# Releasing half of the first weight quarter behind a small copy, and other spins, in the opening of a decayed cumulative sum of a matmul

## The chip, the cores and the metric

The kernel runs on one core of one Trainium2 chip. The metric is the device time of one execution in microseconds, as the median of several runs. TensorE is called PE here, VectorE DVE, ScalarE ACT, GpSimd POOL and SyncE SP. A DMA transfer is issued by SP, ACT or POOL and is carried out by the core's 16 DMA engines; in the profile the queue of POOL is q0, those of SP and ACT are q1 and q10.

## The reference

```python
B, S, D = (16, 2048, 1024)
x = randn(B, S, D)          # float32
w = randn(D, D)             # float32
decay = 0.9 * rand(D) + 0.05

xw = x @ w
out[:, 0, :] = xw[:, 0, :]
for t in range(1, S):
    out[:, t, :] = decay[None, :] * out[:, t - 1, :] + xw[:, t, :]
```

A matrix product with a 1024 x 1024 weight, and then along the time axis a first-order recurrence with one decay for each output channel.

## The kernel before

**Tiling.** The 1024 channels that are summed over are cut into K = 8 blocks of 128, called k. The time axis of each of the 16 batches is cut into 4 chunks of 512 steps, so there are 64 chunks, two to a group. The 1024 output channels are cut into 8 tiles, called n. For each n and chunk the PE sums 8 matmuls of 128x128 weights and 512 columns into PSUM; ACT, DVE and POOL then work out the recurrence with scans, DVE turns the result round by 32x32 transposes, and SP stores it. These steps form one long list that is written out by hand, the agenda; letters stand for deeds, and every instruction is kept in program order on its engine.

**x.** A chunk of x is loaded from POOL with a conversion from float32 to bf16 (L105): four transfers for each piece, one for every quarter q of the channels, each into 32 partitions. Four transposes on DVE (L115, letter E in the opening), one for each m = 0 to 3, bring the channels to the partitions. A transpose delivers a pair of blocks, k = 2m and k = 2m + 1, interleaved. The matmuls of even k read the interleaved tile xw directly at first; those of odd k read a separated copy, xt, made by ACT (G) or DVE (F) at L123.

**w.** The weight is loaded in four quarters (h, e): h is the half of the output channels (0: n = 0 to 3), e the parity of k. A quarter holds the four row sets m = 0 to 3, row set m being block k = 2m + e. The first quarter, (0, 0), is loaded in float32 by two transfers on SP and two on ACT, 256 KB each, one for every channel quarter q, each with all four row sets (`load_w`, L317 to L322). The other three quarters are loaded from POOL with conversion to bf16 (letter U, 128 KB written by each transfer). A row set is then copied, and for the first quarter converted, into its place in wsb by `settle` (L326): letter W on DVE, w on ACT. The numbers 0 to 3 behind these letters are the row sets of (0, 0), 4 to 7 those of (0, 1).

**The opening** (agenda entry -99) runs in this order. POOL issues M0 (x's first chunk, time blocks 0 to 9 of 16), U0 (the second quarter of w), M1 (the rest of x's first chunk), M2 and M3 (the two halves of the second chunk), then U1 and U2 (the third and fourth quarter of w). The order of the other engines' work is that of the agenda's string:

```python
-99: "M0 U0 M1 M2 M3 U1 U2 w0 W1 w2 W3 K3 E0 E1 G0 E2 G1 E3 F2 G3 W4 w5 W6 W7 E4 ...
```

The first real matmuls are those of M0's 320 time steps for n = 0 to 3: sixteen for k = 0, 2, 4, 6, then sixteen for k = 1, 3, 5, 7, and the same for the 192 steps of M1. They need E0 and row set 0 first, then E1 and row set 1, and so on; the odd blocks need U0's row sets (W4, w5, W6, W7) and the copies G and F.

**The spins.** Before any data is there the PE runs matmuls on zeros into a PSUM tile that is overwritten later. `spin(5, seed, wide)` makes five float32 matmuls of 512 columns, each two passes in the profile. Their weights, seed, are zeroed by DVE, and one column of seed is then written by ACT from wide, so the spins start behind that copy. K3 (`spin_on`, L355 to L357) makes one bf16 spin behind the landing of channel quarter 3 of M0: an ACT copy of one column of that quarter into gate, and a matmul with gate as weights.

Of the kernel before, what the change touches and what calls it, by code (L numbers as in the profile page):

```python
# [9 lines left out]
FP32 = mybir.dt.float32  # L10
BF16 = mybir.dt.bfloat16
# [3 lines left out]
def _ap(ap_obj: bass.AP, new_ap, extra_offset=0):  # L15
    return dataclasses.replace(
        ap_obj,
        ap=[list(p) for p in new_ap],
        offset=ap_obj.offset + extra_offset,
    )  # L20
# [5 lines left out]
def kernel(  # L26
# [26 lines left out]
    nc = tc.nc  # L53
    pin = tc.keep_in_program_order
    B, S, D = x.shape
    assert w.shape == (D, D)

    NQ = 4
    P = 32
    CQ = D // NQ  # L60
    K = CQ // P
    M = K // 2
# [3 lines left out]
    R = K // 2  # L66
    CH = D // 2
    CR = CH // NQ

    const = ctx.enter_context(tc.tile_pool(name="const", bufs=1))  # L70
# [9 lines left out]
    def quad(q):  # L80
        return slice(q * P, (q + 1) * P)
# [12 lines left out]
    def ot_tile(nj):  # L94
        return ring(sb, "ot", 4, [128, nj, CR])
# [45 lines left out]
    class Tile:  # L141
# [45 lines left out]
        def copy(self):  # L187
            self.xs = sb.tile([128, 2 * TL], FP32, name=f"xs{self.lot % 3}")[:, 0:self.T]
            size = self.T // len(self.parts())
            for i, ps in enumerate(self.parts()):  # L190
                pin(nc.scalar.copy(out=self.xs[:, i * size:(i + 1) * size], in_=ps))  # L191
# [94 lines left out]
    class Outlet:  # L286
# [8 lines left out]
        def store(self, b, t0):  # L295
# [4 lines left out]
            for j in range(0, self.nj, nj):  # L300
# [8 lines left out]

    room = [ot_tile(2 * NJ).rearrange("p j c -> p (j c)") for _ in range(2)]  # L310
    size = M * CH
    stage = {(0, 0): room[0][:, 0:size],
             (0, 1): room[0][:, size:size * 3 // 2].bitcast(BF16),
             (1, 0): room[1][:, 0:size // 2].bitcast(BF16),
             (1, 1): room[1][:, size // 2:size].bitcast(BF16)}

    def load_w(queues, h, e):  # L317
        for i, q in enumerate((0, 2, 1, 3)):
            pin(queues[i % len(queues)].dma_start(  # L319
                out=stage[h, e][quad(q)].rearrange("p (m d) -> p m d", m=M),  # L320
                in_=_ap(w, [[2 * D, P], [2 * P * D, M], [1, CH]],
                        (q * CQ + e) * D + h * CH)))  # L322

    def settle(h, e, m, copy):
        src = stage[h, e][:, m * CH:(m + 1) * CH]
        pin(copy(out=wcols[:, 2 * m + e, h],  # L326
                 in_=src.rearrange("p (q r i) -> p q r i", q=NQ, r=R)))

    wide = const.tile([128, TL], FP32, name="wide")
    idle = wide[:, 0:TL // 2].bitcast(BF16)  # L330
    spare = ring(psp, "spare", 1, [128, TL])
    rows = const.tile([128, 2, P], FP32, name="rows")
    seed = const.tile([128, 128], FP32, name="seed")
    load_w((nc.sync, nc.scalar), 0, 0)
    pin(nc.vector.memset(wide, 0.0))
    pin(nc.vector.memset(seed, 0.0))
    pin(nc.scalar.copy(out=seed[:, 0:1], in_=wide[:, 0:1]))  # L337

    gate = const.tile([128, 128], BF16, name="gate")
    pin(nc.vector.memset(gate, 0.0))  # L340

    def spin(count, by, on):
        for _ in range(count):
            pin(nc.tensor.matmul(out=spare, lhsT=by, rhs=on, start=True, stop=True))  # L344

    spin(5, seed, wide)
    H = NJ // 2
    cuts = (((0, H + 2), (H + 2, NJ)), ((0, H), (H, NJ)))
    cols = const.tile([128, 2, P], FP32, name="cols")
# [9 lines left out]
    def load_part(i):  # L359
        load_w((nc.gpsimd,), *((0, 1), (1, 0), (1, 1))[i])  # L360
# [4 lines left out]
    def settle_one(i, copy):  # L365
        settle(i // 8, i // 4 % 2, i % 4, copy)
# [119 lines left out]
    def turn_and_load(c):  # L486
# [42 lines left out]
        "L": lambda i: load(*loads.pop(0)) if loads else None,  # L529
    }  # L530
    agenda = {
        -99: "M0 U0 M1 M2 M3 U1 U2 w0 W1 w2 W3 K3 E0 E1 G0 E2 G1 E3 F2 G3 W4 w5 W6 W7 E4 E5 G4 E6 G5 E7 F6 G7 R E8 E9 G8 E10 G9 E11 F10 G11 E12 L E13 G12 L E14 G13 E15 L F14 G15 D",
        0: "",
        1: "",
        2: "",
# [220 lines left out]
```

## Time and profile before

| what | value |
|---|---|
| median of 3 runs | 903.48 us (903.07 to 903.52) |
| the profiled execution | 903.32 us |
| its span, first to last instruction | 901.5 us |
| PE busy | 894.6 us, 4211 matmul records |
| DVE, ACT, POOL busy | 825.8, 685.7, 656.8 us |
| transfers of w's first quarter | 4 x 256 KB, 4.6 us (SP) and 4.9 us (ACT) from issue to landing |
| transfers of M0 | 4 x 160 KB, 6.6 us from issue to landing |
| transfers of w's other quarters | 12 x 128 KB, 5.8 us |

Times are microseconds from the start of the span. A row of the timeline gives the start, the time taken, the engine, the line, the operation, what it writes and reads, how many instructions are merged, and in brackets the idle time ahead of it with what ended it. A row of the windows gives the stretch, its length, the busy time of PE, PE's weight loads, DVE, ACT and POOL with the number of instructions, the granted clock, the share of the DMA engines and their rate in GB/s. A row of a DMA queue gives its packets, the MB written and the time of its packets as a share of the 16 engines' time. x and the later quarters of w are read as float32 and written as bf16, so the bytes read are twice those that the rate shows.

### The profile page before, as it was taken

The page shows a single profiled execution, that of the slowest core. Times are in us where ns is not written, and L with a number is a line of the kernel's source. Part 1 is how long each engine was busy: PE and PEld are TensorE (multiplying, and loading weights), DVE is VectorE, ACT ScalarE, POOL GpSimd, SP SyncE. Part 2 cuts the span into 40 slices and gives each one's busy share as a digit, 9 for nine tenths or more (in the row PEclk, how much of TensorE's full clock was granted, in tenths as well). Part 3 has the DMA queues.
Part 4 walks back from the last instruction along what each step waited for, and adds up shares of the span by engine and source line. Part 5 has one row for each costly group of instructions (what it writes and reads, how often), then busy time and mean ns, then how long its engine had stood idle before and what let it go on. Part 6 is the DMA issues. An engine that isn't in the chain of part 4 may idle for free.

```text
span 901.5 us, 12309 instructions
## 1 busy us (share of the span) xinstructions
PE 894.6 (99%) x4211; PEld 412.8 (46%) x4211; DVE 825.8 (92%) x633; ACT 685.7 (76%) x957; POOL 656.8 (73%) x758
## 2 busy tenths in 40 slices
PE   8999999999999999999999999999999999999998
PEld 5544444444444444444444444444444444444444
DVE  4999989999999999999998999989999999999998
ACT  4888879877877877878778778777787787787743
POOL 7887778877767768677677687777777777776532
PEclk9999999999999999999999999999999999999999
DMA  9999999999999999999999999999999999999658
GB/s 189 192 211 244 244 205 215 215 230 240 248 237 264 242 254 242 256 253 246 220 245 218 228 241 211 239 223 228 236 228 223 229 235 226 230 219 219 187 135 239
DMA packets 403182, 204.77 MB, mean 227 GB/s; under 512 B 9392, under 2 KB 402096, under 8 KB 403120
## 3 DMA queue, kind: packets, MB, share of 16 engines
q0 software_dynamic: 137024, 68.70, 57.5%
q1 hardware_dynamic: 265808, 134.77, 57.1%
q8 instruction: 33, 0.54, 0.2%
q10 hardware_dynamic: 288, 0.52, 0.2%
q14 instruction: 29, 0.24, 0.1%
HBM read 138.42 MB, written 134.22 MB: 302 GB/s over the span
## 4 chain that ended last, share of the span: by engine, by line
PE 99%; ACT 0%; ACTq 0%; DVE 0%; DVEq 0%; issue 0%
PE ps L131 97%; PE spare L131 1%; PE spare L344 1%; ACT L337 0%; PE spare L412 0%; ACTq L319 0%; PE ps L412 0%; DVE h L440 0%; ACT seed L337 0%; DVEq L751 0%
## 5 line engine op out<-in xcount | busy, mean ns | idle before, releaser
L131 PE MATMUL ps<-xt,wsb 128*128 128x512 bf16 (+2 forms) x4040 | 865.9, 377 | 0.0
L131 PEld LDWEIGHTS <-wsb 128*128 128x128 bf16 x4184 | 408.3, 98 | 477.2 <-DVE wsb L326 0.3
L205 POOL TENSOR_TENSOR xs<-h,xs 128x512 f32<-128x512 f32 (+1 forms) x190 | 242.4, 1277 | 185.5 <-ACT h L171 84.4
L191 ACT COPY xs<-ps 128x1024 f32<-128x1024 f32 (+1 forms) x190 | 188.7, 994 | 153.4 <-PE ps L131 147.2
L278 DVE STREAM_TRANSPOSE ot<-so 128x1024 f32<-128x1024 f32 (+2 forms) x264 | 300.6, 1176 | 2.7 <-POOL so L266 2.0
L266 POOL TENSOR_TENSOR so<-h,xs 128x512 f32<-128x512 f32 (+1 forms) x189 | 240.6, 1274 | 38.4 <-ACT h L171 26.2
L123 ACT COPY xt<-xw 128x2048 bf16<-128x2048 bf16 (+3 forms) x136 | 242.4, 1788 | 5.8 <-DVE xw L115 5.8
L105 POOL DMA_DIRECT2D xb<-in_x_dram x264 | 173.8, 659 | 7.6 <-DMA xb<-in_x_dram 2.8
L171 ACT ACTIVATE h<-so,dec 128x512 f32<-128x512 f32 (+1 forms) x189 | 144.7, 766 | 26.6 <-DVE so L210 23.3
L115 DVE STREAM_TRANSPOSE xw<-xb 128x2048 f32<-128x2048 f32 (+3 forms) x78 | 147.2, 1899 | 6.1 <-DMA xb<-in_x_dram 6.1
L210 DVE TENSOR_TENSOR_SCAN so<-spare,keep,xs 128x512 f32<-128x512 f32 (+1 forms) x97 | 120.0, 1240 | 27.5 <-POOL xs L205 26.9
L210 DVE TENSOR_TENSOR_SCAN so<-spare,xs 128x512 f32<-128x512 f32 x93 | 113.3, 1220 | 25.9 <-POOL xs L205 22.6
L171 ACT ACTIVATE h<-ps,dec 128x512 f32<-128x512 f32 (+1 forms) x190 | 129.6, 683 | 0.0
L229 DVE TENSOR_TENSOR_SCAN so<-dec,ps 128x1024 f32<-128x1024 f32 x34 | 76.9, 2261 | 0.8 <-ACT h L171 0.6
L229 DVE TENSOR_TENSOR_SCAN so<-dec,keep,ps 128x1024 f32<-128x1024 f32 (+2 forms) x35 | 75.5, 2156 | 0.8 <-PE ps L131 0.8
L270 ACT COPY keep<-so 128x1 f32<-128x1 f32 x136 | 25.3, 188 | 9.3 <-DVE so L229 8.7
L201 ACT COPY so<-keep 128x1 f32<-128x1 f32 x97 | 18.3, 191 | 3.3 <-DVE ot L278 3.2
L199 POOL MEMSET so<- 128x1 f32 x93 | 10.6, 115 | 3.0 <-DVE ot L278 3.0
L131 PE MATMUL spare<-xt,wsb 128*128 128x512 bf16 (+3 forms) x60 | 12.6, 329 | 0.0
L131 PE MATMUL ps<-xw,wsb 128*128 128x256 bf16 (+3 forms) x72 | 12.2, 306 | 0.0
L344 PE MATMUL spare<-wide,seed 128*128 128x512 f32 x10 | 7.4, 915 | 3.2 <-ACT seed L337 3.2
L319 POOL DMA_DIRECT2D ot<-in_w_dram x12 | 6.5, 548 | 0.7 <-issue 0.3
(43 smaller groups left out, 37.6 us busy)
## 6 DMA issues: line engine op xcount, KB each, us to landing
out_dram<-ot SPq DMA_DIRECT2D x236, 512.0 KB, 8.9
xb<-in_x_dram POOLq DMA_DIRECT2D x248, 256.0 KB, 7.4
out_dram<-ot SPq DMA_DIRECT2D x56, 128.0 KB, 2.2
out_dram<-ot SPq DMA_DIRECT2D x8, 256.0 KB, 4.8
ot<-in_w_dram POOLq DMA_DIRECT2D x12, 128.0 KB, 5.8
xb<-in_x_dram POOLq DMA_DIRECT2D x8, 128.0 KB, 4.5
out_dram<-xb SPq DMA_DIRECT2D x3, 256.0 KB
xb<-in_x_dram POOLq DMA_DIRECT2D x4, 160.0 KB, 6.6
```

What stands on the lines that cost most here:

```text
L105: pin(nc.gpsimd.dma_start(out=xb_of[c][quad(q), j0:j1], in_=_ap(x, [[D, P], [P * D, j1 - j0], [1, CQ]], (b * S + t0 + j0 * P) * D + q * CQ)))
L115: pin(nc.vector.transpose(out=dst.rearrange("p (m j i) -> p j m i", m=M, i=P)[:, j0:j1, m0:m1], in_=src.rearrange("p (j m c) -> p j m c", ...
L123: pin(copy(out=xt_of[c][:, m0:m1, :, j0 * P:j1 * P], in_=src))
L131: return pin(nc.tensor.matmul(out=ps[:, t0 % ps.shape[1]:][:, 0:t1 - t0], lhsT=lhs, rhs=rhs, start=(k == 0 and t0 == start), stop=(k == K ...
L171: pin(nc.scalar.activation(out=h[:, i * size:(i + 1) * size], in_=src, func=mybir.ActivationFunctionType.Copy, scale=dec[:, self.n:self.n ...
L191: pin(nc.scalar.copy(out=self.xs[:, i * size:(i + 1) * size], in_=ps))
L205: pin(nc.gpsimd.tensor_tensor(out=odds, in0=self.g, in1=odds, op=ALU.add))
L210: pin(nc.vector.tensor_tensor_scan(out=so[:, 3:T + 2:2], data0=squares[-1][:, n:n + 1].to_broadcast([128, T // 2]), data1=self.xs[:, 1:T:2 ...
L229: return pin(nc.vector.tensor_tensor_scan(out=so[:, t + 2:t + 2 + size], data0=dec[:, n:n + 1].to_broadcast([128, size]), data1=ps, initia ...
L266: pin(nc.gpsimd.tensor_tensor(out=self.so[:, 2:T + 2:2], in0=self.h, in1=self.xs[:, 0:T:2], op=ALU.add))
L270: pin(nc.scalar.copy(out=self.keep, in_=self.so[:, self.T + 1:self.T + 2]))
L278: pin(nc.vector.transpose(out=outlet.ot[:, :, c0:c0 + P], in_=self.so[:, 2 + t0:2 + t0 + nj * P].rearrange("p (i t) -> p i t", t=P)))
```

## The change

- The loads of the first quarter, (0, 0), are cut in two. Row sets 0 and 1 are issued first, two transfers on SP and two on ACT, of half the size. Row sets 2 and 3 are issued in four more transfers that write the rest of the same tile.
- Between them stands an ACT copy of one zero column from wide into the first column of row set 2's place. The later transfers overwrite that column, so on SP and on ACT they are issued only when the copy is done. The copy takes the place of the one into seed; the tile seed and its memset are gone.
- The spins are four in float32 with `wide[:, 0:128]` as weights, and two in bf16 with gate as weights. They need only DVE's memsets.
- In the agenda K2 is added ahead of K3: one more copy and bf16 spin, behind channel quarter 2 of M0. w2 moves from ahead of K3 to behind K3 on ACT, ahead of G0; W3 moves on DVE from ahead of E0 to behind E3, ahead of F2.

```diff
-    stage = {(0, 0): room[0][:, 0:size],
-             (0, 1): room[0][:, size:size * 3 // 2].bitcast(BF16),
+    early = M // 2
+    rounds = room[0][:, 0:size]
+    stage = {(0, 1): room[0][:, size:size * 3 // 2].bitcast(BF16),
...
-    def load_w(queues, h, e):
+    def staged(h, e, m0, m1):
+        if (h, e) == (0, 0):
+            return rounds[:, m0 * CH:m1 * CH]
+        return stage[h, e][:, m0 * CH:m1 * CH]
+
+    def load_w(queues, h, e, m0=0, m1=M):
         for i, q in enumerate((0, 2, 1, 3)):
             pin(queues[i % len(queues)].dma_start(
-                out=stage[h, e][quad(q)].rearrange("p (m d) -> p m d", m=M),
-                in_=_ap(w, [[2 * D, P], [2 * P * D, M], [1, CH]],
-                        (q * CQ + e) * D + h * CH)))
+                out=staged(h, e, m0, m1)[quad(q)].rearrange("p (m d) -> p m d", m=m1 - m0),
+                in_=_ap(w, [[2 * D, P], [2 * P * D, m1 - m0], [1, CH]],
+                        (q * CQ + e + 2 * P * m0) * D + h * CH)))
 
     def settle(h, e, m, copy):
-        src = stage[h, e][:, m * CH:(m + 1) * CH]
         pin(copy(out=wcols[:, 2 * m + e, h],
-                 in_=src.rearrange("p (q r i) -> p q r i", q=NQ, r=R)))
+                 in_=staged(h, e, m, m + 1).rearrange("p (q r i) -> p q r i", q=NQ, r=R)))
...
-    seed = const.tile([128, 128], FP32, name="seed")
-    load_w((nc.sync, nc.scalar), 0, 0)
+    load_w((nc.sync, nc.scalar), 0, 0, 0, early)
     pin(nc.vector.memset(wide, 0.0))
-    pin(nc.vector.memset(seed, 0.0))
-    pin(nc.scalar.copy(out=seed[:, 0:1], in_=wide[:, 0:1]))
+    pin(nc.scalar.copy(out=rounds[:, early * CH:early * CH + 1], in_=wide[:, 0:1]))
+    load_w((nc.sync, nc.scalar), 0, 0, early, M)
...
-    spin(5, seed, wide)
+    spin(4, wide[:, 0:128], wide)
+    spin(2, gate, idle)
...
-        -99: "M0 U0 M1 M2 M3 U1 U2 w0 W1 w2 W3 K3 E0 E1 G0 E2 G1 E3 F2 G3 W4 w5 W6 W7 E4 ...
+        -99: "M0 U0 M1 M2 M3 U1 U2 w0 W1 K2 K3 E0 E1 w2 E2 E3 W3 G0 G1 F2 G3 W4 w5 W6 W7 E4 ...
```

## The prediction

> **What bounds the kernel now.** I read the shares and the chain first, to see which engine sets the end; then the timeline of the opening; then the half-microsecond windows with the DMA rate, and the queues in single windows.
>
> ```profile
> PE 894.6 (99%) x4211; PEld 412.8 (46%) x4211; DVE 825.8 (92%) x633; ACT 685.7 (76%) x957; POOL 656.8 (73%) x758
> ...
> PE ps L131 97%; PE spare L131 1%; PE spare L344 1%; ACT L337 0%; PE spare L412 0%; ACTq L319 0%; PE ps L412 0%; DVE h L440 0%; ACT seed L337 0%; DVEq L751 0%
> ```
>
> TensorE (PE) is the chain from 3.21 us to the tail. No group of real matmuls has idle time ahead of it that counts, so the end is the start of the first real matmul plus a stream without holes. Only two things can move it: when that stream starts, and holes made in it.
>
> ```profile
> 0.74 0.90 ACTq L319 DMA_DIRECT2D ot<-in_w_dram  x2
> 0.75 0.86 SPq L319 DMA_DIRECT2D ot<-in_w_dram  x2
> ...
> 1.31 2.51 POOL L105 DMA_DIRECT2D xb<-in_x_dram  x4 [0.86 <-POOLq L740]
> ...
> 2.97 0.19 ACT L337 COPY seed<-wide 128x1 f32<-128x1 f32 x1
> ...
> 3.21 7.42 PE L344 MATMUL spare<-wide,seed 128*128 128x512 f32 x10 [3.21 <-ACT seed L337]
> ...
> 7.04 1.14 ACT L326 CAST wsb<-ot 128x512 bf16<-128x512 f32 x2 [3.87 <-DMA ot<-in_w_dram]
> ...
> 10.33 1.69 DVE L115 STREAM_TRANSPOSE xw<-xb 128x320 f32<-128x320 f32 x4 [2.50 <-DMA xb<-in_x_dram]
> ...
> 10.90 0.59 PE L131 MATMUL ps<-xw,wsb 128*128 128x320 bf16 x3
> ...
> 12.94 0.70 DVE L326 COPY wsb<-ot 128x512 bf16<-128x512 bf16 x3 [0.54 <-DMA ot<-in_w_dram]
> ...
> 15.00 1.16 DVE L115 STREAM_TRANSPOSE xw<-xb 128x192 f32<-128x192 f32 x4 [1.36 <-DMA xb<-in_x_dram]
> ```
>
> The reader is to see that the first matmul (10.90) hangs on x's first piece (M0), whose transposes wait for a DMA until 10.33, while w's quarter is there at 7.04, over 3 us before it is needed. Behind it the second quarter of w (12.94) and x's second piece (15.00) also arrive by DMA just when the PE wants them: the hole at 13.29 is 0.15 us, the one at 15.48 nothing. The PE can keep an earlier start only if all these transfers come earlier too.
>
> ```profile
> 3.50:4.00 0.50, 0.50 (x1) 0.21 (x1) 0.00 (x0) 0.00 (x0) 0.50 (x2) 1.00 1.11 377
> 4.00:4.50 0.50, 0.50 (x2) 0.27 (x1) 0.00 (x0) 0.00 (x0) 0.50 (x2) 1.00 0.77 254
> 4.50:5.00 0.50, 0.50 (x1) 0.07 (x1) 0.00 (x0) 0.00 (x0) 0.50 (x2) 1.00 0.83 287
> ...
> 7.00:7.50 0.50, 0.50 (x1) 0.13 (x1) 0.43 (x2) 0.47 (x1) 0.00 (x0) 1.00 1.06 124
> ...
> 8.50:9.00 0.50, 0.50 (x2) 0.33 (x1) 0.00 (x0) 0.00 (x0) 0.20 (x1) 1.00 1.47 196
> ```
>
> The last column is the DMA rate. w runs at 377, dips to 254 and 287 between its two pairs of transfers, and x, alone from 6.5 on, runs at 132, 124, 151 and 160 in four windows before it reaches about 195. By queue, x (q0) moves nothing at all before 5.5, though issued from 1.31 on:
>
> ```profile
> q10 hardware_dynamic: 70, 0.14, 72.6%
> q1 hardware_dynamic: 38, 0.05, 28.6%
> ...
> q0 software_dynamic: 124, 0.06, 92.8%
> ```
>
> (the first two lines are all there is in 5.0 to 5.5, the third is new in 5.5 to 6.0). x starts just as w thins out.
>
> **The change part by part.** *Spins.* They now wait only for the memset of wide (0.92 + 0.48 = 1.40), so they start at about 1.45 instead of 3.21. Before, a pass took 0.85 us until 9.02, some 5.8 us after the first, and 0.43 then. Eight passes with the step 5.8 us after their start: 6.8 x 0.85 + 1.2 x 0.43 = 6.3, so to 7.8; the two bf16 spins at most 0.39 each (the row of the old gate spin), to 8.2 or 8.6. Nothing real waits for them. Their price is nothing as long as the clock stays up until the first real matmul; else see the second rival.
>
> *The copy.* Same instruction, place and 0.19 us, another destination. The removed memset of seed (0.17) had nobody waiting but that copy, which starts behind the table load anyway. Nothing.
>
> *Four more w issues.* Two on ACT behind the copy: 2 x 0.44 from 3.16, to 4.05; ACT then waited until 7.04, so hidden. Two on SP, which waits for the copy: 2 x 0.41; SP's next work is the decay load at 16.5. POOL's queue is not touched. Nothing on either side.
>
> *The moved casts.* On ACT the second cast now stands behind the spin copy at 10.29: 10.5 to 11.1; three copies of 0.66 follow to 13.1 and the next cast (0.62) to 13.7; its matmul ran at 13.85, so 0.13 us to spare. On VectorE (DVE) the fourth cast (0.42) follows the transposes, 12.02 to 12.44, for a matmul at 12.58; the copy behind it ends at 12.89, just ahead of 12.94. Nothing; if these covers were gone, 0.2 us at most (the last ACT cast moves from 12.92 to 13.1). One more spin copy (0.19) and spin (0.39) fall into the wait for x: nothing.
>
> *The transfers* are the one term. The early half of w is 256 packets of 2 KB; summed by quarter microseconds, q1 and q10 had moved 276 packets by 4.0, so it is through at about 3.9. The other half is issued at 3.2; q1's first packet came 1.0 us after its issue and q10's 1.76 us, so it begins at 4.2 and 4.9. That leaves a hole in which x can move, before w's second half joins it. The trace does not show such a hole; its bounds:
> - Gain: what x and w leave unused now. In 4.0 to 5.0, (2 x 375 - 254 - 287) x 0.5 = 104 KB at 375 is 0.28 us. In 6.5 to 8.5, (4 x 195 - 567) x 0.5 = 106 KB at 195 is 0.55 us. Together 0.83. To this the slow first stretch (1.75 to 3.0, 73 packets where the later pace makes 250, some 0.9 us) could add only if restarting cost nothing.
> - Loss: x does not move before 5.5 anyway and w's second half starts as slowly as the first: 73 of its packets by 5.5, 183 left, against about 30 left before. 153 x 2 KB = 0.31 MB, at the 0.39 MB/us that x reads (twice its written 195) 0.8 us if nothing of it fits into the slack of 6.5 to 8.5 (0.55), 0.25 if all does.
>
> I take the gain of 0.83: the nearest row is x's own start, full at once when it comes (18 packets in its first tenth of a microsecond, 40 in its sixth), as of a queue that had been ready and held back. From 8.5 on the same queue carries the second quarter of w and the rest of x at a steady 190 to 207, each transfer let go by the landing of an earlier one, so all arrivals move by the same 0.83 and open no hole.
>
> [...] The trace shows both: 107 packets of q0 beside 105 of q1 in 59.5 to 60.0, and none of q0 beside w before 5.5. This is the third rival's ground.
>
> Sum: the profiled execution took 903.32 (span 901.5 and 1.8 around it); minus 0.83 is 902.49. The median of the runs lies 0.16 above the profiled one: 902.65, called 902.7.
>
> **The rivals.** *1. Restart (the other side).* x starts at 5.5 whatever w does, because it is its own queue that is not ready, and w's second half is then in its way. For it: in 4.0 to 5.0 the engines had room and x took none. Against it: x's full start. Price: the middle of 0.25 and 0.8, +0.5, that is 904.0; it decides from the point where more than 30 w packets are left when x starts.
>
> *2. Clock.* Spins end at about 8.2; x's third landing, which lets the added spin go, came at about 9.2 (issued 2.6, landed 6.6 later), the fourth at 10.1 (3.2 and 6.9); both by 0.8 earlier in the forecast. The PE thus idles in pieces of 0.5 to 1.5 us where before it had one of 0.4. If the clock falls back, the first real matmuls run at half speed until it is up again, 5.8 us by the spins' row: 2.9 lost. On top of the forecast: +2.1, 905.6. Against it: no row here shows a fall. [...]
>
> *3. It changes nothing.* w's second half joins the queue before x gets a turn, or the queues only trade places: +0, 903.5.
>
> *4. Late w.* As x stood behind w, w's second half stands behind x and even behind the next quarter on x's queue. It then lands at about 12.6 with its cast to 13.2, where its matmul ran at 12.02; the matmuls behind come at 14.3 instead of 13.29: +1.0, 904.5. For it: the total hold of one queue over the other before 5.5. Against it: the equal sharing at 59.5.
>
> **How the numbers follow.** Forecast 0.42 (own range 902.0 to 903.3), restart 0.20, clock 0.18, nothing 0.10, late w 0.10. The bar of 0.2% is 1.8 us, about what a measurement of this kernel can tell from no change: 901.67 and 905.29. Faster than that needs 0.83 and all of the slow first stretch: 0.06. Slower: three quarters of the clock (0.14), a third of late w, and a little of restart: 0.19. Within: 0.75. The range runs from 901.9, the forecast with half as much again, to 905.6, the clock's price; beyond it lie half of the clock case and the outer tails.
>
> **What would show it.** Right: q0 packets from about 4.0; the first transposes at about 9.5 and the first real matmul at 10.1 in place of 10.90; second quarter's cast at 12.1, x's second piece at 14.2; no hole in the PE's row. Wrong: q0 still silent to 5.5 (restart, nothing); 320-column matmuls 0.27 us apart instead of 0.14 (clock); a wait of the PE for the moved casts (late w). A start that moves while the arrivals at 12.94 and 15.00 stay would show up as holes and no gain.

## The result and the profile after

The changed kernel took 906.02 us in the median of 12 runs (904.02 to 908.05), the kernel before 903.48 (902.75 to 904.65, 12 runs): a ratio of 1.0028 with a 95% interval of 1.0018 to 1.0038. It is slower by 2.5 us, where 0.8 less was forecast. It also scatters: the three runs with a mean clock of 0.999 or 1.000 took 904.0 to 904.6, the five at 0.997 or 0.998 took 905.4 to 906.3, the four at 0.996 took 907.2 to 908.1. The profiled execution took 905.84 with a span of 904.1, that is 2.6 longer than the span before.

The chain of the changed kernel by engine, on the page:

```profile
PE 98%; DMA 1%; POOL 0%; issue 0%; DVE 0%; ACT 0%; DVEq 0%; ACTq 0%; POOLq 0%
```

and some of its first pieces in order of time (start, time taken, what):

```profile
1.31 1.92 POOL xb L105 x3
3.23 7.79 DMA xb<-in_x_dram
...
11.34 0.39 PE spare L348
11.73 0.91 PE ps L131 x3
```

The fp32 spins are no longer on it; of the spins only the one behind x's last channel quarter (11.34) is. The end now hangs on the last transfer of x's first piece, 7.79 us from issue to landing, and on the PE behind it. The timeline of the opening:

```profile
0.75 3.28 SPq L325 DMA_DIRECT2D ot<-in_w_dram  x4
...
1.46 5.42 PE L348 MATMUL spare<-wide 128*128 128x512 f32 x8 [1.46 <-DVE wide L339]
...
3.19 0.85 ACTq L325 DMA_DIRECT2D ot<-in_w_dram  x2
...
6.71 0.59 PE L348 MATMUL spare<-wide,gate 128*128 128x512 bf16 x2
...
9.80 0.39 PE L348 MATMUL spare<-wide,gate 128*128 128x512 bf16 x1 [2.50 <-ACT gate L361]
...
11.14 1.69 DVE L115 STREAM_TRANSPOSE xw<-xb 128x320 f32<-128x320 f32 x4 [5.90 <-DMA xb<-in_x_dram]
...
11.34 0.39 PE L348 MATMUL spare<-wide,gate 128*128 128x512 bf16 x1 [1.15 <-ACT gate L361]
...
11.71 0.94 PE L131 MATMUL ps<-xw,wsb 128*128 128x320 bf16 x3
...
15.79 1.16 DVE L115 STREAM_TRANSPOSE xw<-xb 128x192 f32<-128x192 f32 x4 [1.35 <-DMA xb<-in_x_dram]
```

Two things to see. The first transposes start at 11.14 instead of 10.33, and the first real matmul at 11.71 instead of 10.90: 0.81 late. And three matmuls of 320 columns take 0.94 where they took 0.59, behind holes of the PE of 2.50 and 1.15 us. The windows show why; the last three columns are the granted clock, the DMA share and GB/s:

```profile
3.50:4.00 0.50, 0.50 (x2) 0.17 (x1) 0.00 (x0) 0.00 (x0) 0.50 (x2) 1.00 0.96 124
...
5.50:6.00 0.50, 0.50 (x3) 0.26 (x2) 0.00 (x0) 0.00 (x0) 0.48 (x1) 1.00 1.07 127
...
7.50:8.00 0.50, 0.00 (x0) 0.00 (x0) 0.00 (x0) 0.00 (x0) 0.37 (x1) 1.00 1.02 241
...
11.50:12.00 0.50, 0.50 (x3) 0.19 (x2) 0.50 (x3) 0.50 (x2) 0.44 (x2) 0.78 1.25 199
12.00:12.50 0.50, 0.50 (x4) 0.26 (x3) 0.50 (x3) 0.50 (x2) 0.50 (x1) 0.50 1.30 193
...
15.00:15.50 0.50, 0.50 (x5) 0.30 (x3) 0.00 (x0) 0.00 (x0) 0.50 (x2) 0.81 1.44 192
```

The clock is at half from about 11.8 to 15.2. The first sixteen real matmuls took 15.57 - 11.71 = 3.86 us to the start of the next block; before, 13.29 - 10.90 = 2.39 with a wait of 0.15 in it, which is gone in the changed kernel. So the profiled execution lost 0.81 by the late start and, with that wait set against it, 1.47 by the clock, 2.28 in all; from 27.7 us to the last DVE work the distance to before stays at 2.23 to 2.24, and 0.36 more lies behind that work, at the very end. Where x moves, by queue (packets, MB, share of the engines), first in 3.25 to 3.50, then in 6.00 to 6.25:

```profile
q0 software_dynamic: 18, 0.01, 26.9%
...
q1 hardware_dynamic: 3, 0.01, 20.4%
```

x does start in the hole, at about 3.3 instead of 5.5. But from 4.0 to 6.0, alone on the engines, it runs at only 126 to 163 GB/s, and w's second half, issued from 3.19 on, brings its first packet only at 6.0, and its last after 10.2.

### The profile page after: what moved, and what is told of

Same layout as the page of the kernel before. It is cut to its first block, busy times and chain, and to the rows that moved or that the text cites. A ratio compares the mean times of both kernels' runs of the same rounds, so it can differ in the third digit from the quotient of the medians.

```text
span 904.1 us, 12321 instructions
## 1 busy us (share of the span) xinstructions
PE 895.0 (99%) x4212; PEld 413.0 (46%) x4212; DVE 825.8 (91%) x632; ACT 685.8 (76%) x958; POOL 657.7 (73%) x758
## 4 chain that ended last, share of the span: by engine, by line
PE 98%; DMA 1%; POOL 0%; issue 0%; DVE 0%; ACT 0%; DVEq 0%; ACTq 0%; POOLq 0%
PE ps L131 97%; PE spare L131 1%; DMA xb<-in_x_dram 1%; POOL xb L105 0%; PE spare L417 0%; PE ps L417 0%; DVE h L445 0%; PE spare L348 0%; ACT gate L361 0%; DVEq L756 0%; ACTq L361 0%; POOLq L745 0%
## 5 line engine op out<-in xcount | busy, mean ns | idle before, releaser
L348 PE MATMUL spare<-wide 128*128 128x512 f32 x8 | 5.4, 836 | 1.5 <-DVE wide L339 1.5
```

## The experiments

Each kernel is the changed one but for the edit shown, unless it says otherwise. "Clock low" counts the executions with a mean clock of 0.998 or less; none of the 86 executions of the kernel before that ran beside these kernels was so low. The last column is that of one execution, the profiled one.

| kernel | median us | range | clock low | first transposes, in its profile |
|---|---|---|---|---|
| before | 903.3 to 903.5 | 902.8 to 904.7 | 0 of 86 | 10.33 |
| changed | 906.02 | 904.0 to 908.1 | 9 of 12 | 11.14 |
| 14 early spins | 904.72 | 904.1 to 905.6 | 0 of 11 | 11.85 |
| whole loads | 903.43 | 903.1 to 904.8 | 3 of 11 | 10.27 |
| old spins | 905.23 | 904.5 to 906.8 | 1 of 11 | 10.63 |
| divided, no wait | 904.92 | 904.3 to 906.6 | 0 of 11 | 12.30 |
| agenda alone | 903.45 | 902.9 to 903.9 | 0 of 11 | 10.14 |
| one spin fewer | 906.12 | 905.7 to 907.7 | 5 of 5 | 10.98 |
| second half behind x | 910.73 | 909.2 to 911.5 | 5 of 5 | 9.23 |
| second half on POOL | 905.97 | 905.5 to 906.8 | 3 of 6 | 9.99 |
| whole loads, 12 spins | 904.05 | 903.3 to 904.3 | 0 of 11 | 10.30 |
| released by DVE | 906.08 | 904.8 to 906.4 | 5 of 6 | 11.37 |
| full-size transfers | 904.82 | 904.1 to 905.8 | 0 of 11 | 11.56 |
| late spins | 905.24 | 904.4 to 907.8 | 3 of 11 | 12.25 |

**14 early spins: the hole filled.**

```diff
-    spin(2, gate, idle)
+    spin(14, gate, idle)
```

> The changed kernel with 14 bf16 spins in place of 2, so that the PE works on until about 9.9 us instead of 7.3. Theory (two costs that add: the clock falls because the PE idles from 7.3 to 9.8 and from 10.2 to 11.3, and x's first piece lands 0.8 us late because w's held-back half comes in beside it): the granted clock stays at 1.00 from the first real matmul on, the first piece still lands late (transposes at about 11.1), so 904.3, and the scatter of 904.0 to 908.1 closes to that of the kernel before. Rival (the clock falls for another reason, the early start of the spins for one): 906.0 and the same scatter.

904.72, a ratio of 1.0013 (1.0004 to 1.0022) to before. The PE's rows:

```profile
6.76 3.19 PE L348 MATMUL spare<-wide,gate 128*128 128x512 bf16 x14
...
10.51 0.39 PE L348 MATMUL spare<-wide,gate 128*128 128x512 bf16 x1 [0.57 <-ACT gate L361]
...
12.41 0.58 PE L131 MATMUL ps<-xw,wsb 128*128 128x320 bf16 x3
```

The work ends at 9.95, the first real matmuls take 0.58 although they begin even later, and no execution has a low clock. So, by the medians, 906.02 - 904.72 = 1.3 of the loss is the clock, and 904.72 - 903.5 = 1.2 is left with the clock up. The three executions of the changed kernel that kept the clock took 904.0 to 904.6; by their middle one, 904.26, it would be 1.8 and 0.8. Which of the two is nearer is not shown: x may have come early in those three, or the added spins may cost something themselves.

**Whole loads: the changed spins without the divided loads.**

```diff
-    load_w((nc.sync, nc.scalar), 0, 0, 0, early)
+    load_w((nc.sync, nc.scalar), 0, 0)
+    seed = const.tile([128, 1], FP32, name="seed")
...
-    pin(nc.scalar.copy(out=rounds[:, early * CH:early * CH + 1], in_=wide[:, 0:1]))
-    load_w((nc.sync, nc.scalar), 0, 0, early, M)
+    pin(nc.scalar.copy(out=seed, in_=wide[:, 0:1]))
```

> The changed kernel's spins and agenda, but w's first quarter is loaded whole and at once as before; the small copy goes to a tile of its own. Theory: x's first piece lands at 10.3 as before, and the PE idles from about 7.3 to 9.4 and 9.8 to 10.5, so the clock falls in many of the executions: 903.5 to 906.9 with a median near 905, scattered. Rival (the held-back half is what costs, through DMA alone): 903.5 and no scatter.

The hole and the first transposes:

```profile
9.66 0.39 PE L348 MATMUL spare<-wide,gate 128*128 128x512 bf16 x1 [2.63 <-ACT gate L361]
...
10.27 1.69 DVE L115 STREAM_TRANSPOSE xw<-xb 128x320 f32<-128x320 f32 x4 [2.73 <-DMA xb<-in_x_dram]
```

903.43, ratio 1.0003 (0.9994 to 1.0011): x is on time, and the whole loss of the median is gone. Three of eleven executions had a clock of 0.998, all at 904.7 to 904.8, the profiled one among them (its windows from 12 to 14 us stand at 0.50). So the spins make the clock fall without the loads too, but less often than expected: the holes are 2.63 and 0.41 us here, and the median stays.

**Old spins: the divided loads with the PE at work.**

```diff
+    seed = const.tile([128, 128], FP32, name="seed")
...
+    pin(nc.vector.memset(seed, 0.0))
...
+    pin(nc.scalar.copy(out=seed[:, 0:1], in_=wide[:, 0:1]))
...
-    spin(4, wide[:, 0:128], wide)
-    spin(2, gate, idle)
+    spin(5, seed, wide)
```

> The changed kernel's loads and agenda, with the five fp32 spins of before behind their own ScalarE copy, from about 3.4 us on. Theory: the PE works until about 10.7, the clock stays at 1.00, and only the late first piece is left: 904.3, no scatter. Rival (everything lies in the clock, and x's lateness was that one execution): 903.5. Rival (smaller transfers or the moved casts cost more than that): 905 or more with the clock at 1.00.

905.23, ratio 1.0020 (1.0011 to 1.0028), nearly a microsecond more than expected with the clock up in ten of eleven. In its profile x was early for a divided load (10.63), but the copy behind the last quarter had to wait for the added spin, which stood behind the fp32 spins until 11.1. That explains a part in that one execution; the rest of the run's scatter was not taken apart.

**Divided, no wait.** Eight transfers at once, the changed agenda, the spins of before.

```diff
+    seed = const.tile([128, 128], FP32, name="seed")
     load_w((nc.sync, nc.scalar), 0, 0, 0, early)
+    load_w((nc.sync, nc.scalar), 0, 0, early, M)
     pin(nc.vector.memset(wide, 0.0))
-    pin(nc.scalar.copy(out=rounds[:, early * CH:early * CH + 1], in_=wide[:, 0:1]))
-    load_w((nc.sync, nc.scalar), 0, 0, early, M)
+    pin(nc.vector.memset(seed, 0.0))
+    pin(nc.scalar.copy(out=seed[:, 0:1], in_=wide[:, 0:1]))
...
-    spin(4, wide[:, 0:128], wide)
-    spin(2, gate, idle)
+    spin(5, seed, wide)
```

> The loads cut in two, but all eight transfers are issued at once with no copy to wait for; the changed kernel's agenda, the spins of before. Theory (it is the wait, not the cut, that delays x): x's first piece lands at 10.3, 903.5. Rival (eight small transfers are slower than four, or the agenda costs): 904.3, as in the run that keeps the wait.

904.92, ratio 1.0017 (1.0009 to 1.0026): the expected 903.5 did not come. The first transposes, and the queues in 4.0 to 4.5:

```profile
12.30 1.69 DVE L115 STREAM_TRANSPOSE xw<-xb 128x320 f32<-128x320 f32 x4 [6.91 <-DMA xb<-in_x_dram]
...
q0 software_dynamic: 37, 0.02, 32.1%
q1 hardware_dynamic: 10, 0.02, 25.8%
q10 hardware_dynamic: 8, 0.01, 6.6%
```

All eight transfers were issued by 2.6, yet by queue only the first two of SP and of ACT ran ahead of x. x moved from 3.5 on, and the other four trickled in beside it: 18 packets in 4.0 to 4.5, 23 in the next half microsecond. The wait is not needed for the harm: here x got in between although all of w's first quarter had been issued, as four smaller transfers on each queue in place of two. The profiled execution (906.17) is one of the slower ones of this kernel.

**Agenda alone**, on the kernel before.

```diff
-        -99: "M0 U0 M1 M2 M3 U1 U2 w0 W1 w2 W3 K3 E0 E1 G0 E2 G1 E3 F2 G3 W4 ...
+        -99: "M0 U0 M1 M2 M3 U1 U2 w0 W1 K2 K3 E0 E1 w2 E2 E3 W3 G0 G1 F2 G3 W4 ...
```

> The kernel before with nothing but the changed agenda: the added copy and spin behind channel quarter 2, and the two moved casts. Theory (the agenda costs nothing by itself): 903.5, x's first piece at 10.3. Rival (the 1.2 to 1.7 us that the runs with divided loads and an unbroken clock lost lie in the moved casts): 904.7 or more.

903.45, ratio 1.0000 (0.9991 to 1.0009). The moved casts, the added copy and spin cost nothing.

**One spin fewer.**

```diff
-        -99: "... w0 W1 K2 K3 E0 E1 ...
+        -99: "... w0 W1 K3 E0 E1 ...
```

> The changed kernel without the added copy and spin behind channel quarter 2, so that the PE idles in one piece from 7.3 to about 11.3. Theory (the length of the idle time decides on the clock): the clock falls in every execution or nearly, and later executions lose up to 3.4 us at half speed: median 906.5 to 907.5, none below 905. Rival (the clock falls whatever the PE does in that time): the same 906.0 and scatter as the changed kernel.

906.12, and every one of five executions at a clock of 0.997 or less, none below 905.66; the hole is 4.21 us. The median is a little under what was expected. In the profiled execution, the fastest of the five, the clock is at half for 3.41 us; the two at 0.996 took 907.5 and 907.7, which fits twice that.

**Second half behind x.** It is released by the landing of x's first piece.

```diff
-    pin(nc.scalar.copy(out=rounds[:, early * CH:early * CH + 1], in_=wide[:, 0:1]))
-    load_w((nc.sync, nc.scalar), 0, 0, early, M)
...
-    spin(2, gate, idle)
+    spin(6, gate, idle)
...
+    def load_late(i):
+        pin(nc.scalar.copy(out=rounds[:, early * CH:early * CH + 1], in_=xb_of[0][:, 0, 0:1]))
+        load_w((nc.sync, nc.scalar), 0, 0, early, M)
...
-        -99: "... W1 K2 K3 E0 ...
+        -99: "... W1 K2 K3 N0 E0 ...
```

> The changed kernel, but w's second half is released only by the landing of all of x's first piece, and there are six bf16 spins. Theory (x is late because w's second half comes in beside it from 6 us on): with x alone on the engines its first piece lands before 10.3, about 9.2, so the first transposes start then; w's second half is then late and the PE waits for its casts, until about 12. Rival (x is late because its own queue starts slowly, whatever comes beside it): transposes at 10.5 or later here too.

Three rows of the timeline and two of the windows:

```profile
9.23 1.69 DVE L115 STREAM_TRANSPOSE xw<-xb 128x320 f32<-128x320 f32 x4 [3.94 <-DMA xb<-in_x_dram]
...
9.62 0.85 ACTq L325 DMA_DIRECT2D ot<-in_w_dram  x2
...
15.83 0.62 ACT L331 CAST wsb<-ot 128x512 bf16<-128x512 f32 x1 [6.24 <-DMA ot<-in_w_dram]
...
4.00:4.50 0.50, 0.50 (x2) 0.32 (x1) 0.00 (x0) 0.00 (x0) 0.50 (x2) 1.00 1.09 137
...
7.50:8.00 0.50, 0.50 (x4) 0.10 (x1) 0.00 (x0) 0.00 (x0) 0.30 (x1) 1.00 1.45 190
```

With x alone its first piece is there at 9.23, 1.1 sooner than before, as expected: it is w's second half beside it that makes x late. But that half, issued at 9.6, was cast at 15.83, not at 12, its first packets coming from about 11.9 on. 910.73: the PE waited 5.4 us, and the clock fell in that wait. SP's first packet of the held half came some 2.3 us after its issue here and ACT's 2.9, against 2.8 and 3.7 in the changed kernel and 1.0 and 1.8 for the first transfers of the kernel before.

**Second half on POOL**, converted on the way, between x's first piece and the second quarter.

```diff
-    pin(nc.scalar.copy(out=rounds[:, early * CH:early * CH + 1], in_=wide[:, 0:1]))
-    load_w((nc.sync, nc.scalar), 0, 0, early, M)
...
-    spin(2, gate, idle)
+    spin(6, gate, idle)
...
+    def load_late(i):
+        load_w((nc.gpsimd,), 0, 0, early, M)
...
-        -99: "M0 U0 M1 ...
+        -99: "M0 N0 U0 M1 ...
```

> The changed kernel with w's second half moved to POOL's queue, behind x's first piece and ahead of the second quarter of w, converted on the way, with six bf16 spins. Theory (one queue in the wanted order does what the change was to do): x's first piece at about 9.2, w's second half by about 10.3, the first real matmul near 9.8; but the second quarter and the rest of x still come through the same engines, so the PE meets holes and the whole gains 0.2 to 0.8: 902.7 to 903.3. Rival (x cannot come earlier): 903.5 or more. Rival (four more transfers on POOL delay the ones behind them, since each waits for an earlier one to land): 904 or more.

905.97. x's first piece came at 9.99, but the last rival held: in the timeline the first eight POOL transfers were issued by 5.9, and each of the four of the second quarter only as one of x's transfers landed (7.59, 8.41, 9.27, 10.15), the DMA rate sank to 116 GB/s in 12 to 13 us, and the PE waited for that quarter:

```profile
10.15 0.54 POOL L327 DMA_DIRECT2D ot<-in_w_dram  x1 [0.33 <-DMA xb<-in_x_dram]
...
15.12 0.62 ACT L333 COPY wsb<-ot 128x512 bf16<-128x512 bf16 x1 [1.32 <-DMA ot<-in_w_dram]
...
15.50 0.58 PE L131 MATMUL ps<-xt,wsb 128*128 128x320 bf16 x3 [1.14 <-DVE wsb L333]
```

No version here beats the kernel before.

**Whole loads, 12 spins.** The run with whole loads, with `spin(12, gate, idle)`.

> Whole loads of w's first quarter at once and the changed agenda, with 12 bf16 spins in place of 2. In the run with two the clock was below 1.00 in some executions and the median was that of the kernel before. Theory (the hole in the PE's work from 7.0 to 9.7 lets the clock fall in some executions): no execution above 904.3 now, median 903.4, clock 1.00 or 0.999 everywhere. Rival (the early start of the spins costs the clock): the same four or so executions of eleven at 904.3 to 904.8.

904.05, ratio 1.0006 (0.9997 to 1.0015). No low clock any more, as expected, so the early start of the spins alone does not make the clock fall. But the spins were too many: in the profile the clock rose late, the fp32 spins took 6.51 us where the changed kernel's took 5.42, the bf16 spins ran to 10.56, and the first real matmul came at 11.74 with x ready at 10.30.

**Released by DVE**, 1.5 us sooner.

```diff
-    pin(nc.scalar.copy(out=rounds[:, early * CH:early * CH + 1], in_=wide[:, 0:1]))
+    pin(nc.vector.tensor_copy(out=rounds[:, early * CH:early * CH + 1], in_=wide[:, 0:1]))
```

> The changed kernel with the small copy made by VectorE at about 1.5 us instead of ScalarE at 3.0, so that w's second half is issued some 1.5 us sooner. Theory (the wait is not what decides: x gets in between the halves as soon as there are two on each queue, as in the run without any wait): x moves from 3.3 on and its first piece is as late as there or in the changed kernel, transposes at 11 to 12.3, and the clock falls as in the changed kernel: 905 to 907. Rival (it depends on who is issued first: w's second half now stands ahead of x): x at 5.5 and its first piece at 10.3, 903.5 to 905.

906.08, x from 3.3 on, transposes at 11.37, the clock low in five of six: as without a wait for the loads, and as in the changed kernel for the clock.

**Full-size transfers.** All four row sets in each, but two of the four transfers held behind the copy; casts behind x, 14 spins.

```diff
-    load_w((nc.sync, nc.scalar), 0, 0, 0, early)
+    load_w((nc.sync, nc.scalar), 0, 0, qs=(0, 2))
...
-    pin(nc.scalar.copy(out=rounds[:, early * CH:early * CH + 1], in_=wide[:, 0:1]))
-    load_w((nc.sync, nc.scalar), 0, 0, early, M)
+    for q in (1, 3):
+        pin(nc.scalar.copy(out=rounds[quad(q), 0:1], in_=wide[quad(q), 0:1]))
+    load_w((nc.sync, nc.scalar), 0, 0, qs=(1, 3))
...
-    spin(2, gate, idle)
+    spin(14, gate, idle)
...
-        -99: "... w0 W1 K2 K3 E0 E1 ...
+        -99: "... K2 K3 E0 w0 W1 E1 ...
```

> Transfers of full size, all four row sets each, but two of the four (channel quarters 1 and 3 of w) are held behind the small copy; the first casts stand behind the landing of x, and 14 bf16 spins keep the PE at work. Theory (what costs is that w's second half comes in beside x, not that the transfers are small): x moves from about 3.4 on, w's held transfers begin at about 6, x's fourth landing is at 11.0 or later as in the runs with half-size transfers. Rival (small transfers are what costs): x's fourth landing at 10.3 or sooner. The time itself has about 0.6 more for the first casts, which here stand between x and the first real matmul.

The first of the transposes:

```profile
11.56 0.51 DVE L115 STREAM_TRANSPOSE xw<-xb 128x320 f32<-128x320 f32 x1 [10.08 <-DMA xb<-in_x_dram]
```

904.82. x moved from 3.4 on, and its last landing let the transposes go only at 11.56. So small transfers are not needed for the harm; x getting between the two parts of w is what these runs have in common. The held transfers began earlier than expected, between 4.0 and 4.5 (SP) and between 5.5 and 6.0 (ACT), and still x was late.

**Late spins.** Eight spins behind the landing of channel quarter 2 instead of one.

```diff
-        spin(1, gate, idle)
+        spin(8 if q == 2 else 1, gate, idle)
```

> The changed kernel with eight bf16 spins in place of one behind the landing of channel quarter 2, about 9.8 to 11.6 us; the PE's hole from 7.3 to 9.8 stays as it is. Theory (the clock is decided at the ends of fixed stretches of 3.41 us, by how busy the PE was in the stretch: in the runs so far it fell behind stretches of 0 to 45% and stayed behind those of 56% and more): the stretch from about 8.4 to 11.8 is now some 58% busy, the clock stays at 1.00 in most executions, and the time is that of the run with 14 early spins plus some 0.3 for the spins that hold up the last ones: 905.0. Rival (a hole of 2.5 us by itself makes the clock fall, some time later): clock 0.997 and 906 or more, as in the changed kernel.

905.24. Eight of eleven executions kept the clock at 0.999 or 1.000, at 904.4 to 906.0, against three of twelve in the changed kernel, though the hole ahead of the spins was not filled. The profiled execution (907.49) is one of the other three: x was later there, its spins began only at 10.91, and the clock fell at 11.63, before they could count.

## Why the prediction was wrong

**What bounds the kernel** held for the start of the real matmuls and for holes in their stream. It named only these two; the speed of the stream, which the second rival brought in, took 1.47 us of the profiled execution.

**The spins** were mis-sized, and the second rival, which hung on them, was right that the clock would fall. The step said that the clock rises 5.8 us after the first pass, so that the spins end at 8.2 and leave pieces of 0.5 to 1.5 us. It rose at 4.97, 3.5 us after, the spins ended at 7.3, and the holes were 2.50 and 1.15. The 5.8 was the row of one execution: in the fourteen profiles here the rise came 2.87 to 6.05 us after the first pass. Nine of twelve executions show a low clock. The rival's price of 2.9 was too high for the profiled one (1.47), where the clock is low for 3.41 us and not 5.8. It was about right for the four at 0.996: they lie 2.9 to 3.8 above the middle one of the three with the clock up. No profile of one of them was kept; "second half behind x", also at 0.996, shows the clock low from 15.21 to 22.04, twice as long. Against the rival stood that no row of the kernel before shows a fall; that pieces of 0.5 to 1.5 us cost nothing was shown by no row there either. In the changed kernel the clock fell behind 2.50 and 1.15 with a spin between them, and was low from 11.78 to 15.19.

**The transfers** are the step that failed. It was right that x would use the hole: its first packets came at 3.3, forecast 4.0. It failed at "I take the gain of 0.83". The two slack stretches were to fill each other. But x's slow running is its own, not that of the time: alone, it made 126 to 163 GB/s from 4.0 to 6.0, where before it had made 124 to 160 from 6.5 to 8.5, so the slow stretch moved along. In "second half behind x" it made 98 to 155 from 4.0 to 7.5 and 183 and more only behind that. Why x starts slowly is open. And w's second half, which was to fill the stretch from 4.2 on, had its first packet at 6.0 and ran beside x when x was to run full. x landed 0.81 late in place of 0.83 early; with w's half kept away it landed at 9.23, 1.1 sooner than before. The median keeps a loss of 0.8 to 1.2 with the clock up. The loss bound of 0.8 had the size by luck, since its mechanism, x silent until 5.5, did not happen; the restart rival was wrong for the same reason, and so was the third rival.

**Late w**, the fourth rival, named half of the mechanism: w's second half did stand behind x. It did not reach the PE as a wait for its casts, since x itself was later. Where x was early, in "second half behind x", it did, with 5.4 us.

**The copy, the added issues and the moved casts at nothing**: right for the moved casts (903.45 for the agenda alone) and for a copy in that place (903.43 with the changed spins and whole loads). The added issues were not run by themselves; in the timeline ACT's end at 4.04, ahead of its cast at 4.78, and SP's at 4.03, with nothing to do until 17.29.

**The range** ended at 905.6 because it took either the clock or the transfers to go wrong. Both did: 0.8 to 1.2 for the late x and 1.3 to 1.8 for the clock, together the 2.5. That 905.6 lies near the measured 906.02 is chance: it puts x 0.83 early and the clock at 2.9.

## What to carry to other kernels

Holding back a transfer does not only give its place to another: it has to get in again, and beside x's queue that took 1.3 to 4.2 us here. Of the orders tried, none beat the one in which the four whole loads are issued first and run to their end. If a stretch of low DMA rate is to be filled, find out first whether the slowness is that of the time or of the queue that runs in it. Spins that are to keep the clock up were too few, or too late, in six profiles of the table below (the PE busy for 0 to 45% of the 3.41 us ahead of the clock's fall), and enough with 14 of them (56% from 8.44 to 11.85 in the profiled execution, no low clock in eleven). They must not run past the first real work in the execution in which they go slowest, as the 12 spins did (first real matmul at 11.74, x ready at 10.30).

## What had not been expected of the hardware

**The clock fell 6.80 to 6.82 us after its rise, once 10.22.** In the changed kernel a pass of the fp32 spins took 0.85 us at first (2.48 to 3.33) and 0.43 later (5.00 to 5.43). From the pass between, the time of the rise is estimated: with 0.82 (4.18 to 5.00) it was slow for 2 x 0.82 - 0.85 = 0.79, so the clock rose at 4.97. It fell at 11.78, found from windows of 0.2 us. In the seven profiles with a fall:

| kernel | rise | fall | fall - rise | PE busy in the 3.41 us ahead of the fall |
|---|---|---|---|---|
| one spin fewer | 4.33 | 11.13 | 6.80 | 0% |
| late spins | 4.83 | 11.63 | 6.80 | 21% |
| changed | 4.97 | 11.78 | 6.81 | 24% |
| released by DVE | 5.38 | 12.20 | 6.82 | 30% |
| whole loads | 4.41 | 11.22 | 6.81 | 34% |
| second half on POOL | 4.49 | 11.30 | 6.81 | 45% |
| second half behind x | 4.99 | 15.21 | 10.22 | 0% |

In the changed kernel the clock came back 3.41 later (15.19 - 11.78). The distances in the table are twice that, and in the last row three times, wherever the holes lie. In the last row it came back only 6.83 later, at 22.04; the 3.41 us behind that fall, with the PE idle until 16.50, were 62% busy, and the clock stayed at half behind them:

```profile
15.00:15.50 0.50, 0.00 (x0) 0.00 (x0) 0.00 (x0) 0.00 (x0) 0.00 (x0) 0.71 1.47 197
...
22.00:22.50 0.50, 0.50 (x6) 0.32 (x4) 0.50 (x2) 0.50 (x2) 0.50 (x2) 0.96 1.25 202
```

With 14 early spins the rise was at about 5.03, the stretch from 8.44 to 11.85 by the same count was 56% busy, and the clock stayed; so did it behind the stretch from 4.97 to 8.38 of the changed kernel, which was 68% busy. So in these profiles the clock fell behind stretches with 0 to 45% and stayed behind those with 56% and 68%; the holes at or ahead of a fall go from 5.42 us (second half behind x) to 1.40 and 0.46 (second half on POOL). Counted back from the rise in the same way, a stretch of 84% (one spin fewer, 0.92 to 4.33) was followed by it, and one of 77% (old spins, 2.54 to 5.95) was not. That the share decides, and where between these figures, is not shown. The rise differs from one execution to the next (4.33 to 7.25 behind the same first pass at 1.46, the latest in the run with full-size transfers), which fits the scatter of the changed kernel.

**Spins of 0.85 us a pass show a clock of 1.00.** In the changed kernel the windows' clock column says 1.00 from 1.5 to 4.5 us, where passes take 0.85 us, as from 5.0 on, where they take 0.43. Only the fall and the return from it are shown there (0.50 in 12.0 to 15.0).

**The held part of w had its first packet 1.3 to 4.2 us after its issue.** In the seven profiles with a held part of w, the first packet of that part came 1.3 to 3.9 us after its issue on SP and 2.8 to 4.2 us on ACT, while x's queue ran; at the start of the kernel before it was 1.0 and 1.8. Why is open; no run issued them late with x's queue at rest. Also open is why x lands late although the number of its queue's packets moved by 9.5 us is about the same as before (1281 in place of 1292). In the changed kernel that queue's packets of 4.0 to 9.0 hold 0.5 KB on the average, those of 9.0 to 10.0 0.6, and those of 10.0 to 11.0, ahead of the last landing of x's first piece at 11.02, 0.9. The kernel before shows the same averages in these stretches, and its transposes start at 10.33.
